# Encoder layer, second FFN matrix: a block that leaves later, a gate inside an operand, and a last row block in two half banks

## The chip, the cores and the metric

The kernel runs on one core of a Trainium2 chip. The metric is the device time of one execution in microseconds (us). Five engines have queues of their own: PE multiplies matrices, ACT and DVE work elementwise and read PE's banks, POOL works elementwise on SBUF, and SP issues all the transfers that matter here. PEld in the rows is PE's loading of weights.

## The reference

One encoder layer: conditioning by six modulation rows, two attention branches, a gated merge, and then the part that the change touches. With `h2` the modulated norm of `x`:

```
a, up = jnp.split(h2 @ w_ffn_in[l], 2, axis=-1)
x = x + gt2 * ((jax.nn.silu(a) * up) @ w_ffn_out[l])
```

`x` is 1024 x 1024, the inner width D_FF is 2816, `gt2` is one row of 1024 gates that multiplies each row. All is float32.

## The kernel before

The products are done in pieces: a float32 operand is split into a rounded part `whi` (copied by ACT, line 107) and the rest `wlo` (subtracted by DVE or POOL, line 108), and three matmuls per pair of operands (hi-hi, hi-lo, lo-hi, `PASS`) make up one product. The function `wsplit` does that for an operand of 128x512; `wload` (line 100) loads one into one of six buffers `raw`. There are ten buffers each for `whi` and `wlo`.

The second FFN matrix, `[silu(a)*up] @ w_ffn_out`, is a 2x2 block product with 7 block products instead of 8. `PRODS` lists them; `prod2(n)` does product n, with n from 0 to 6 here. Each sums over 11 steps k; a step takes an operand a (a combination of the activations, from `ga_d`) and an operand b (a block of the weights or a mix of blocks), and does 4 row blocks m x 3 passes = 12 matmuls of 512 columns, so 132 in a product. The four sums of a product lie in four banks, of the tags `d` and `s` for even products and `v` and `t` for odd ones, two banks to a tag.

Products 0, 1 and 2 use blocks of `w_ffn_out` as they are; DVE subtracts both parts `wlo` for them. During products 1 and 2 `w2_mix(k)` also loads all four blocks of step k again (line 1336) and DVE makes the mixes of them (lines 1338 to 1341), 44 subtractions in all, for products 3 to 6. From product 3 on POOL subtracts most of the `wlo` of operand b. Product 6 uses the fourth mix (`m3` in the program, made in line 1341). Its last three steps (`LASTK`) are done row block by row block, so that the four sums are ready one after the other.

What a product gives is added into four output blocks c11, c12, c21, c22 of four tiles 128x512 each. A block that is ready is finished by `finish`: a load of the residual from `x2_d` (line 1382), a multiplication by the gate on DVE (line 1383), an addition of the residual on POOL (line 1384) and a store (line 1386). c11 is ready after product 1 and is finished there. c21 gets its gate and residual ahead of product 6, which is still missing in it; product 6 is then multiplied by the gate out of its banks and added (lines 1418, 1419), and stored (line 1420).

PE's order is that of the program. The order on ACT, DVE, POOL and SP is made by a scheduler when the program is built: it takes what is ready in its own timeline, by the order of the program as priority. Each engine then runs its queue strictly in order.

Of the kernel before, what the change touches and what calls it, by code (L numbers as in the profile page):

```python
# [10 lines left out]
F32 = mybir.dt.float32  # L11
# [30 lines left out]
def hybrid_layer(ctx: ExitStack, tc: tile.TileContext, x, colp, wada1, wada2, bada2, wqkv, wg, wpa, wpb,  # L42
                 wo, w1, w2, hgain, ropeg, rope, rbias, bmask, g2r, out):
    nc = tc.nc

    def pool(name, side, **kw):
        return tc.alloc_tile_pool(name=name, bufs=1, side=side, reuse_waits="tile", **kw)
# [19 lines left out]
    def bank(tag):  # L67
        return ps.tile([128, 512], F32, tag=tag, name="ps_" + tag)
# [26 lines left out]
    def fview(ap):  # L95
        return ap.bitcast(F32)

    def wload(src, n):
        raw = wp.tile([128, 512], F32, tag="raw", bufs=NRAW, name="raw")
        nc.sync.dma_start(raw[:, :n], src)  # L100
        return raw[:, :n]

    def wsplit(r, eng=None):
        n = r.shape[1]
        hi = wp.tile([128, 512], F32R, tag="hi", bufs=NHL, name="whi")
        lo = wp.tile([128, 512], F32R, tag="lo", bufs=NHL, name="wlo")
        nc.scalar.activation(hi[:, :n], r, AF.Copy)  # L107
        (eng or nc.gpsimd).tensor_sub(lo[:, :n], r, fview(hi[:, :n]))  # L108
        return hi, lo
# [1113 lines left out]
    cs = {}  # L1223
# [100 lines left out]
    fp = pool("f2", "left")  # L1324
    gt2 = fp.tile(wide, F32, name="gt2")
    nc.sync.dma_start(gt2, mod_d[3072:4096].rearrange("(o n) -> o n", o=1).to_broadcast([128, 1024]))
    def w2blk(r, c, k):
        return w2[(k + HT * r) * 128:(k + HT * r + 1) * 128, c * 512:c * 512 + 512]
# [4 lines left out]
    def w2_mix(k):  # L1333
        b = [w2p.tile([128, 512], F32, name=f"m{n}_{k}") for n in range(4)]
        for z, (r, c) in zip(b, ((0, 0), (0, 1), (1, 1), (1, 0))):
            pin(nc.sync.dma_start(z, w2blk(r, c, k)))
        t1, t3, t2, t4 = b
        nc.vector.tensor_sub(t1, t3, t1)  # L1338
        nc.vector.tensor_sub(t3, t2, t3)  # L1339
        nc.vector.tensor_sub(t2, t2, t1)  # L1340
        nc.vector.tensor_sub(t4, t4, t2)  # L1341
        w2m[k] = t1, t2, t3, t4

    PRODS = ((0, (0, 0)), (1, (1, 0)), (6, (1, 1)), (4, 1), (3, 0), (5, 2), (2, 3))
    LASTK = 3

    def operands(n, k):
        g, m = PRODS[n]
        a = wload(ga_d[g, k], 512)
        b = w2m[k][m] if n > 2 else wload(w2blk(*m, k), 512)  # L1350
        return wsplit(a, nc.vector), wsplit(b, nc.vector if n < 3 or k == HT - 1 or (n == 6 and k > 4) else None)

    def blocks(name):
        return [fp.tile([128, 512], F32, name=f"{name}{m}") for m in range(4)]

    def prod2(n):
        pb = [bank(("ds", "vt")[n % 2][m // 2]) for m in range(4)]
        last = LASTK if n == 6 else 0

        def mm(k, m, o):  # L1360
            for i, (a, b) in enumerate(PASS):
                nc.tensor.matmul(pb[m], o[0][a][:, m * 128:(m + 1) * 128], o[1][b],  # L1362
                                 start=(k == 0 and i == 0), stop=(k == HT - 1 and i == 2))

        for k in range(HT - last):
            o = operands(n, k)
            if n in (1, 2) and k % 2 == n - 1:
                w2_mix((k + (n - 1) * HT) // 2)
            for m in range(4):
                mm(k, m, o)  # L1370
        ops = {k: operands(n, k) for k in range(HT - last, HT)}
        for m in range(4):
            for k in ops:
                mm(k, m, ops[k])
        return pb

    def finish(rh, c, z, last=None):
        cs = slice(c * 512, c * 512 + 512)
        for m in range(4):
            t = rh * 4 + m  # L1380
            xt = fp.tile([128, 512], F32, tag="x2", bufs=4, name="x2")
            nc.sync.dma_start(xt, x2_d[t * 128:(t + 1) * 128, cs])
            nc.vector.tensor_mul(z[m], z[m], gt2[:, cs])
            nc.gpsimd.tensor_add(z[m], z[m], xt)
            if last is None:
                nc.sync.dma_start(out[t * 128:(t + 1) * 128, cs], z[m])

    c11, c12, c21, c22 = (blocks(z) for z in ("c11", "c12", "c21", "c22"))
    add = nc.vector.tensor_add
    p1 = prod2(0)  # L1390
    for m in range(4):
        nc.scalar.activation(c21[m], p1[m], AF.Copy)
    p2 = prod2(1)
    for m in range(4):
        add(c11[m], c21[m], p2[m])  # L1395
    finish(0, 0, c11)
    p3 = prod2(2)
    for m in range(4):
        add(c12[m], c21[m], p3[m])
    p6 = prod2(3)  # L1400
    for m in range(4):
        add(c21[m], c21[m], p6[m])
        add(c12[m], c12[m], p6[m])
    p5 = prod2(4)
    for m in range(4):
        add(c22[m], c21[m], p5[m])
# [6 lines left out]
    finish(1, 1, c22)  # L1413
    finish(1, 0, c21, True)
    p4 = prod2(6)
    for m in range(4):
        tm = fp.tile([128, 512], F32, tag="tm", bufs=4, name="tmf")
        nc.vector.tensor_mul(tm, p4[m], gt2[:, :512])
        nc.vector.tensor_add(tm, tm, c21[m])
        nc.sync.dma_start(out[(m + 4) * 128:(m + 5) * 128, :512], tm)  # L1420
    w2p.release()
    fp.release()
    ps.release()
# [102 lines left out]
```

## Time and profile before

| | |
|---|---|
| median of 3 runs | 1542.0 us (1538.08 to 1543.08) |
| the profiled execution's own time | 1540.34 us |
| its span, first to last instruction | 1538.5 us |
| granted TensorE clock, mean | 0.999 of full |
| busy | PE 98%, DVE 72%, ACT 44%, POOL 35% |

The trace has a time for each instruction of one execution. Times are counted from the span's start; a row gives the start, the length, the engine, the line of the program and the tiles it writes and reads. Where an engine stood idle before an instruction, the row ends with how long and with what ended it. PE's matmuls overlap, so their starts tell the pace, not their lengths.

### The profile page before, as it was taken

How to read it: one execution, taken by the hardware profiler on the slowest of the kernel's cores; microseconds unless marked ns; L12 is line 12 of the kernel's file. 1: busy time of each engine (PE TensorE's matmuls, PEld its weight loads, DVE VectorE, ACT ScalarE, POOL GpSimd, SP SyncE). 2: the span in 40 equal slices, each digit the busy share in tenths (PEclk: the TensorE clock that was granted, in tenths of full speed). 3: DMA queues.
4: the chain of work that ended last, by engine and by line, in shares of the span. 5: the costliest groups of instructions: out<-in, count | busy, mean ns of one | idle time of the engine just before them, and what ended most of it. 6: DMA issues, size and time to landing. Idle time of an engine off the chain costs nothing. (4 is left out here: it accounts for less than half of the span.)

```text
span 1538.5 us, 24632 instructions
## 1 busy us (share of the span) xinstructions
PE 1513.6 (98%) x8156; PEld 1268.2 (82%) x8156; DVE 1109.3 (72%) x2428; ACT 671.3 (44%) x1719; POOL 531.8 (35%) x540
## 2 busy tenths in 40 slices
PE   9999999999999999999999999999999999999998
PEld 7988898988888877788888888888888888887886
DVE  6867786776889855466665497788767775599468
ACT  5555654555555453245532344233233333344442
POOL 0422331321000030001361211677777775104464
PEclk9999999999999999999999999999999999999999
DMA  9615355552354354833553235345443334798342
GB/s 366 231 47 177 106 160 163 172 170 83 104 149 131 107 172 138 299 120 117 171 169 139 86 105 179 112 135 178 156 132 103 107 111 131 256 357 284 104 151 103
DMA packets 158016, 241.67 MB, mean 157 GB/s; under 512 B 27312, under 2 KB 77360, under 8 KB 157120
## 3 DMA queue, kind: packets, MB, share of 16 engines
q1 hardware_dynamic: 156736, 235.90, 47.0%
q10 hardware_dynamic: 1152, 4.19, 0.7%
q8 instruction: 65, 1.06, 0.3%
q14 instruction: 63, 0.52, 0.1%
HBM read 179.89 MB, written 60.15 MB: 156 GB/s over the span
## 5 line engine op out<-in xcount | busy, mean ns | idle before, releaser
L107 ACT ACTIVATE whi<-raw 128x512 fp32r<-128x512 f32 (+1 forms) x348 | 205.0, 601 | 300.5 <-PE ps_s L1362 40.6
L108 POOL TENSOR_TENSOR wlo<-raw,whi 128x512 fp32r<-128x512 f32 (+2 forms) x133 | 168.9, 1282 | 473.1 <-ACT whi L107 323.8
L292 PE MATMUL ps_d<-whi,hT 128*128 128x384 f32 x1152 | 317.5, 343 | 1.3 <-ACT v L327 1.3
L108 DVE TENSOR_TENSOR wlo<-raw,whi 128x512 fp32r<-128x512 f32 (+1 forms) x215 | 184.3, 868 | 79.3 <-ACT whi L107 74.6
L292 PEld LDWEIGHTS ps_d<-whi,hT 128*128 128x128 f32 x1152 | 211.0, 188 | 7.0 <-ACT vs L330 2.6
L292 PE MATMUL ps_d<-wlo,hT 128*128 128x384 f32 x576 | 193.9, 337 | 0.4 <-POOL wlo L108 0.4
L292 PEld LDWEIGHTS ps_d<-wlo,hT 128*128 128x128 f32 x576 | 108.8, 189 | 0.7 <-POOL wlo L108 0.7
L107 ACT ACTIVATE whi<-ws 128x512 fp32r<-128x512 f32 x65 | 41.0, 631 | 123.9 <-DVE ws L1209 47.4
L1142 POOL TENSOR_TENSOR e<-e,c 128x512 f32<-128x512 f32 x44 | 68.2, 1549 | 66.3 <-DVE c L1272 40.3
L322 POOL TENSOR_TENSOR ra<-qn,rtab 128x64 f32<-128x64 f32 x48 | 16.8, 349 | 170.8 <-DVE qn L315 144.0
L456 ACT ACTIVATE P<-P,st 128x256 f32<-128x256 f32 (+2 forms) x100 | 46.1, 462 | 58.5 <-DVE st L455 58.5
L108 POOL TENSOR_TENSOR wlo<-m,whi 128x512 fp32r<-128x512 f32 x35 | 51.9, 1493 | 54.6 <-ACT whi L107 54.5
L599 PE MATMUL ps_d<-hT,whi 128*128 128x512 f32 x192 | 60.5, 396 | 0.0
L1192 PE MATMUL ps_v<-h2T,whi 128*128 128x512 f32 x192 | 59.3, 390 | 0.0
L1192 PE MATMUL ps_s<-h2T,whi 128*128 128x512 f32 x192 | 59.2, 390 | 0.0
L456 ACT ACTIVATE P<-P,sx 128x384 f32<-128x384 f32 (+1 forms) x64 | 37.1, 580 | 48.0 <-DVE sx L455 48.0
L441 PE MATMUL ps_s<-qk 64*128 64x256 f32 (+3 forms) x492 | 53.8, 321 | 3.3 <-DVE qk L371 2.0
L1192 PE MATMUL ps_d<-h2T,whi 128*128 128x512 f32 x184 | 56.9, 390 | 0.0
L313 DVE TENSOR_REDUCE ss<-sq 128x4 f32<-128x256 f32 x80 | 33.1, 414 | 32.6 <-ACT sq L310 32.5
L441 PEld LDWEIGHTS ps_s<-qk 64*128 64x128 f32 (+1 forms) x492 | 35.0, 182 | 25.2 <-issue 13.2
L482 PE MATMUL ps_v<-PT,v 128*64 128x128 f32 (+1 forms) x672 | 54.6, 284 | 0.8 <-DVE PT L471 0.8
L108 DVE TENSOR_TENSOR wlo<-ws,whi 128x512 fp32r<-128x512 f32 x45 | 49.4, 1098 | 8.2 <-ACT whi L107 8.2
(436 smaller groups left out, 3989.6 us busy)
## 6 DMA issues: line engine op xcount, KB each, us to landing
raw<-in_w_dram SPq DMA_DIRECT2D x139, 256.0 KB
ga_d<-e SPq DMA_DIRECT2D x77, 256.0 KB
raw<-ga_d SPq DMA_DIRECT2D x77, 256.0 KB
wa<-in_wada_dram SPq DMA_DIRECT2D x32, 512.0 KB
raw<-in_wqkv_dram SPq DMA_DIRECT2D x80, 192.0 KB
m<-in_w_dram SPq DMA_DIRECT2D x44, 256.0 KB
raw<-in_wg_dram SPq DMA_DIRECT2D x42, 256.0 KB
xt<-in_x_dram SPq DMA_DIRECT2D x16, 512.0 KB
```

Of the source, the lines that this page charges most:

```text
L107: nc.scalar.activation(hi[:, :n], r, AF.Copy)
L108: (eng or nc.gpsimd).tensor_sub(lo[:, :n], r, fview(hi[:, :n]))
L292: nc.tensor.matmul(pd[:, :384], tok(a, k, t), U.w[k][b][:, :384], start=(k == 0 and i == 0), stop=(k == KT - 1 and i == 2))
L313: nc.vector.tensor_reduce(ss, sq.rearrange("p (h d) -> p h d", h=4), axis=mybir.AxisListType.X, op=ALU.add)
L322: nc.gpsimd.tensor_tensor(v4(ra), v4(qn[:, :, 0:16]), tv(0, 0, 16), op=ALU.mult)
L441: nc.tensor.matmul(I.pS[h][:nq, :nk], U.qk[a][hs, I.q0:I.q0 + nq], U.qk[2 + b][hs, I.kb0 * 128:I.kb0 * 128 + nk], start=(i == 0), stop=(i ...
L456: nc.scalar.activation(P[:nq, :nk], P[:nq, :nk], AF.Exp, scale=-1.0, bias=nm, accum_out=sm)
L482: nc.tensor.matmul(po[hs, :nq], U.v[:, I.kb0 + i, hs], I.PT[h][:, i, :nq], start=(i == 0), stop=(i == nkb - 1))
L599: nc.tensor.matmul(st["p"], gw[i, br][j][a][:, kk * 128:(kk + 1) * 128], hT[b][:, k, hs], start=(k == 0 and q == 0), stop=(k == 7 and q == 2))
L1142: nc.gpsimd.tensor_mul(sg, sg, up)
L1192: nc.tensor.matmul(pb, w[p][:, k * 128:(k + 1) * 128], b[q][:, k], start=(k == 0 and i == 0), stop=(k == 3 and i == 2))
```

## The change

It makes three edits in the second FFN matrix. `finish(0, 0, c11)` is written after product 3's additions instead of after product 1's. Operand b of product 6 is multiplied by the gate before it is split, 11 multiplications of 128x512 on DVE; the four multiplications of product 6's banks by the gate go, and its banks are added straight into c21. The fourth row block of product 6 is summed as two halves of 256 columns in two banks, the second of the tag `v`, with an addition and a store each. Lines below the edits move by 5 to 7.

```diff
     def operands(n, k):
         g, m = PRODS[n]
         a = wload(ga_d[g, k], 512)
         b = w2m[k][m] if n > 2 else wload(w2blk(*m, k), 512)
+        if n == 6:
+            nc.vector.tensor_mul(b, b, gt2[:, :512])
         return wsplit(a, nc.vector), wsplit(b, nc.vector if n < 3 or k == HT - 1 or (n == 6 and k > 4) else None)
...
         last = LASTK if n == 6 else 0
-
-        def mm(k, m, o):
+        whole = slice(0, 512)
+        cuts = [(m, whole, pb[m]) for m in range(4)]
+        if last:
+            pb.append(bank("v"))
+            cuts[3:] = [(3, HALF[h], pb[3 + h][:, HALF[h]]) for h in range(2)]
+
+        def mm(k, m, o, cs, p):
             for i, (a, b) in enumerate(PASS):
-                nc.tensor.matmul(pb[m], o[0][a][:, m * 128:(m + 1) * 128], o[1][b],
+                nc.tensor.matmul(p, o[0][a][:, m * 128:(m + 1) * 128], o[1][b][:, cs],
                                  start=(k == 0 and i == 0), stop=(k == HT - 1 and i == 2))
...
-            for m in range(4):
-                mm(k, m, o)
+            for m, cs, p in cuts:
+                mm(k, m, o, cs, p)
...
-    finish(0, 0, c11)
     p3 = prod2(2)
...
         add(c21[m], c21[m], p6[m])
         add(c12[m], c12[m], p6[m])
+    finish(0, 0, c11)
     p5 = prod2(4)
...
     p4 = prod2(6)
-    for m in range(4):
-        tm = fp.tile([128, 512], F32, tag="tm", bufs=4, name="tmf")
-        nc.vector.tensor_mul(tm, p4[m], gt2[:, :512])
-        nc.vector.tensor_add(tm, tm, c21[m])
-        nc.sync.dma_start(out[(m + 4) * 128:(m + 5) * 128, :512], tm)
+    for m, hs, p in [(m, slice(0, 512), p4[m]) for m in range(3)] + [(3, HALF[h], p4[3 + h]) for h in range(2)]:
+        add(c21[m][:, hs], c21[m][:, hs], p[:, hs])
+        nc.sync.dma_start(out[(m + 4) * 128:(m + 5) * 128, hs], c21[m][:, hs])
```

How the queues move. First DVE at the start of product 2, before the change. The tiles `c_15030` to `c_15033` are c11, `gt` is the gate, `m_7` and its like are the mixes of step 7:

```order
L1395 TENSOR_TENSOR c_15030<-c_15038,ps_v 128x512
L108 TENSOR_TENSOR wlo<-raw,whi 128x512
L1395 TENSOR_TENSOR c_15031<-c_15039,ps_v 128x512
L108 TENSOR_TENSOR wlo<-raw,whi 128x512
L1383 TENSOR_TENSOR c_15030<-c_15030,gt_15025 128x512
L1395 TENSOR_TENSOR c_15032<-c_15040,ps_t 128x512
L108 TENSOR_TENSOR wlo<-raw,whi 128x512
L1395 TENSOR_TENSOR c_15033<-c_15041,ps_t 128x512
L1383 TENSOR_TENSOR c_15031<-c_15031,gt_15025 128x512
L108 TENSOR_TENSOR wlo<-raw,whi 128x512
L1338 TENSOR_TENSOR m_7_15782<-m_7_15783,m_7_15782 128x512
L1383 TENSOR_TENSOR c_15032<-c_15032,gt_15025 128x512
```

And the same place with the change, where line 1383 has become 1390 and 1395 has become 1402:

```order
L1402 TENSOR_TENSOR c_15031<-c_15039,ps_v 128x512
L108 TENSOR_TENSOR wlo<-raw,whi 128x512
L1390 TENSOR_TENSOR c_15030<-c_15030,gt_15025 128x512
L1402 TENSOR_TENSOR c_15032<-c_15040,ps_t 128x512
L108 TENSOR_TENSOR wlo<-raw,whi 128x512
L1402 TENSOR_TENSOR c_15033<-c_15041,ps_t 128x512
L108 TENSOR_TENSOR wlo<-raw,whi 128x512
L1352 TENSOR_TENSOR m_6_15705<-m_6_15705,gt_15025 128x512
L1390 TENSOR_TENSOR c_15031<-c_15031,gt_15025 128x512
L1338 TENSOR_TENSOR m_7_15762<-m_7_15763,m_7_15762 128x512
L1390 TENSOR_TENSOR c_15032<-c_15032,gt_15025 128x512
L108 TENSOR_TENSOR wlo<-raw,whi 128x512
```

The multiplications of c11 by the gate stand where they stood, and one of the eleven new ones (line 1352) stands among them.

Second, DVE at the end of product 2, where the mixes of the last step are made; before the change:

```order
L1338 TENSOR_TENSOR m_10_15962<-m_10_15963,m_10_15962 128x512
L1339 TENSOR_TENSOR m_10_15963<-m_10_15964,m_10_15963 128x512
L1340 TENSOR_TENSOR m_10_15964<-m_10_15964,m_10_15962 128x512
L1341 TENSOR_TENSOR m_10_15965<-m_10_15965,m_10_15964 128x512
L108 TENSOR_TENSOR wlo<-raw,whi 128x512 x3
L1399 TENSOR_TENSOR c_15034<-c_15038,ps_d 128x512
```

With the change:

```order
L1338 TENSOR_TENSOR m_10_15942<-m_10_15943,m_10_15942 128x512
L1339 TENSOR_TENSOR m_10_15943<-m_10_15944,m_10_15943 128x512
L1340 TENSOR_TENSOR m_10_15944<-m_10_15944,m_10_15942 128x512
L1341 TENSOR_TENSOR m_10_15945<-m_10_15945,m_10_15944 128x512
L108 TENSOR_TENSOR wlo<-raw,whi 128x512
L1352 TENSOR_TENSOR m_10_15945<-m_10_15945,gt_15025 128x512
L108 TENSOR_TENSOR wlo<-raw,whi 128x512 x2
L1405 TENSOR_TENSOR c_15034<-c_15038,ps_d 128x512
```

The first two `wlo` here are the two parts of product 2's step 10, the third is product 3's; the last of the new multiplications stands between the two. The other ten stand ahead of it, one behind each set of mixes.

Third, the end of DVE's queue, before the change and with it:

```order
L1418 TENSOR_TENSOR tmf<-ps_s,gt_15025 128x512
L1419 TENSOR_TENSOR tmf<-tmf,c_15040 128x512
L1418 TENSOR_TENSOR tmf<-ps_s,gt_15025 128x512
L1419 TENSOR_TENSOR tmf<-tmf,c_15041 128x512
L1522 UNCONDITIONAL_BRANCH
```

```order
L1424 TENSOR_TENSOR c_15039<-c_15039,ps_d 128x512
L1424 TENSOR_TENSOR c_15040<-c_15040,ps_s 128x512
L1424 TENSOR_TENSOR c_15041<-c_15041,ps_s 128x256
L1424 TENSOR_TENSOR c_15041<-c_15041,ps_v 128x256
L1527 UNCONDITIONAL_BRANCH
```

Two operations per row block become one, and the last row block's one becomes two of half the width.

## Rows read from the trace of the kernel before

**Rows 1.** The page's second part: DVE's busy tenths in 40 slices.

```profile
DVE  6867786776889855466665497788767775599468
```

**Rows 2.** Timeline of PE, product 2 (start us, length us, what): start, hole, end.

```profile
1378.20 0.39 PE L1362 MATMUL ps_d<-whi 128*128 128x512 f32 x1
1378.43 0.39 PE L1362 MATMUL ps_d<-wlo,whi 128*128 128x512 f32 x1
...
1392.57 0.50 PE L1362 MATMUL ps_d<-wlo,whi 128*128 128x512 f32 x1 [3.09 <-DVE wlo L108]
...
1410.06 0.50 PE L1362 MATMUL ps_d<-wlo,whi 128*128 128x512 f32 x1
...
1412.72 0.39 PE L1362 MATMUL ps_v<-whi 128*128 128x512 f32 x1
```

**Rows 3.** Windows: length, then PE, PEld, DVE, ACT, POOL, clock, DMA share, GB/s.

```profile
1342.00:1378.00 36.00, 36.00 (x161) 29.80 (x160) 32.74 (x51) 15.61 (x26) 0.00 (x0) 1.00 1.01 363
1378.00:1413.00 35.00, 31.56 (x135) 24.63 (x133) 32.98 (x48) 13.55 (x23) 7.21 (x5) 1.00 0.94 331
```

**Rows 4.** Timelines of POOL and DVE in product 2.

```profile
1385.74 1.68 POOL L1384 TENSOR_TENSOR c<-c,x 128x512 f32<-128x512 f32 x1 [1.82 <-DVE c L1383]
...
1386.18 1.78 DVE L1338 TENSOR_TENSOR m<-m,m 128x512 f32<-128x512 f32 x1
...
1394.24 0.68 DVE L1338 TENSOR_TENSOR m<-m,m 128x512 f32<-128x512 f32 x1
1394.84 0.68 DVE L1340 TENSOR_TENSOR m<-m,m 128x512 f32<-128x512 f32 x1
```

**Rows 5.** The same timelines at the seam of products 2 and 3.

```profile
1408.72 1.28 DVE L108 TENSOR_TENSOR wlo<-raw,whi 128x512 fp32r<-128x512 f32 x2
...
1412.71 1.20 DVE L108 TENSOR_TENSOR wlo<-raw,whi 128x512 fp32r<-128x512 f32 x1
...
1412.07 3.00 POOL L108 TENSOR_TENSOR wlo<-m,whi 128x512 fp32r<-128x512 f32 x2 [20.11 <-ACT whi L107]
```

**Rows 6.** Timeline of DVE, products 1 and 2: every idle stretch over 0.2 us.

```profile
1347.82 0.69 DVE L1338 TENSOR_TENSOR m<-m,m 128x512 f32<-128x512 f32 x1 [1.25 <-DMA m<-in_w_dram]
...
1353.13 0.69 DVE L1338 TENSOR_TENSOR m<-m,m 128x512 f32<-128x512 f32 x1 [0.28 <-DMA m<-in_w_dram]
...
1374.67 1.96 DVE L108 TENSOR_TENSOR wlo<-raw,whi 128x512 fp32r<-128x512 f32 x3 [1.17 <-ACT whi L107]
...
1404.57 1.36 DVE L108 TENSOR_TENSOR wlo<-raw,whi 128x512 fp32r<-128x512 f32 x2 [0.25 <-ACT whi L107]
```

**Rows 7.** Waits of SP, 1330 to 1415: total us, times, longest.

```profile
SPq L100 <- DVE wlo L108: 11.3, 17, 1.5
```

**Rows 8.** Timeline at 153 us, scores of one item; then their group (ns of one).

```profile
153.06 0.41 PEld L441 LDWEIGHTS ps_s<-qk 64*128 64x128 f32 x6 [0.25 <-issue]
153.06 0.62 PE L441 MATMUL ps_s<-qk 64*128 64x256 f32 x6
...
L441 PE MATMUL ps_s<-qk 64*128 64x256 f32 x228 | 23.9, 314 | 2.0 <-DVE qk L371 2.0
```

**Rows 9.** Line 1362: weight loads of one kind, ns min/median/max.

```profile
L1362 PEld LDWEIGHTS ps_s<-whi,wlo x88: 187/188/188, 1320.0 to 1533.3; 128*128 128x128 f32 x88
```

**Rows 10.** Timeline of PE and DVE where product 6 begins.

```profile
1503.12 0.39 PE L1362 MATMUL ps_d<-whi 128*128 128x512 f32 x1
...
1503.50 0.68 DVE L1412 TENSOR_TENSOR c<-c,ps_v 128x512 f32<-128x512 f32 x1
```

**Rows 11.** Timeline, the end of the span.

```profile
1533.57 0.39 PE L1362 MATMUL ps_s<-whi,wlo 128*128 128x512 f32 x1
...
1534.00 0.69 DVE L1418 TENSOR_TENSOR tmf<-ps_s,gt 128x512 f32<-128x512 f32 x1 [0.18 <-PE ps_s L1362]
1534.79 0.69 DVE L1419 TENSOR_TENSOR tmf<-tmf,c 128x512 f32<-128x512 f32 x1
```

**Rows 12.** Groups of DVE: 128x256 out of a bank, busy us, mean ns.

```profile
L455 DVE CUSTOM_DVE_ANT_0 P<-ps_s,bmask 128x256 f32<-128x256 f32 x60 | 23.5, 418 | 1.8 <-PE ps_s L441 1.0 <-PE ps_t L467 0.3
```

More of the change, by code (lines that the diff above doesn't have):

```diff
@@ L1344, in hybrid_layer @@
     PRODS = ((0, (0, 0)), (1, (1, 0)), (6, (1, 1)), (4, 1), (3, 0), (5, 2), (2, 3))
-    LASTK = 3
+    LASTK, HALF = 3, (slice(0, 256), slice(256, 512))
     def operands(n, k):
@@ L1368, in prod2 @@
                 w2_mix((k + (n - 1) * HT) // 2)
-            for m in range(4):
-                mm(k, m, o)
+            for m, cs, p in cuts:
+                mm(k, m, o, cs, p)
         ops = {k: operands(n, k) for k in range(HT - last, HT)}
-        for m in range(4):
+        for m, cs, p in cuts:
             for k in ops:
-                mm(k, m, ops[k])
+                mm(k, m, ops[k], cs, p)
         return pb
@@ L1415, in hybrid_layer @@
     p4 = prod2(6)
-    for m in range(4):
-        tm = fp.tile([128, 512], F32, tag="tm", bufs=4, name="tmf")
-        nc.vector.tensor_mul(tm, p4[m], gt2[:, :512])
-        nc.vector.tensor_add(tm, tm, c21[m])
-        nc.sync.dma_start(out[(m + 4) * 128:(m + 5) * 128, :512], tm)
+    for m, hs, p in [(m, slice(0, 512), p4[m]) for m in range(3)] + [(3, HALF[h], p4[3 + h]) for h in range(2)]:
+        add(c21[m][:, hs], c21[m][:, hs], p[:, hs])
+        nc.sync.dma_start(out[(m + 4) * 128:(m + 5) * 128, hs], c21[m][:, hs])
     w2p.release()
```

## Prediction

> **What bounds the kernel now.** The page comes first: DVE, otherwise far from full, reaches nine tenths in two neighbouring slices late in the run [rows 1]; PE is busy throughout. Busy share says little of PE here, because matmuls overlap; the starts do. In the second FFN matrix a 512-column matmul starts about 0.227 us after the one before it (1378.20, 1378.43), so one product of 132 matmuls takes 132 x 0.227 = 29.9 us when nothing is late. Product 2 starts at 1378.20 and product 3 at 1412.72: 34.5 us, so PE lost 4.6 us in it, 3.1 of them in one hole before 1392.57, whose releaser is DVE's `wlo` [rows 2]. Second view, the windows: in the two stretches ahead of product 2 and in it DVE is busy for over 90%, the DMA engines for 94% or more, and PE's clock is granted in full [rows 3]. Product 2 is therefore set by DVE and the loads it shares a loop with, not by PE; products 3 to 5 are PE alone; and behind the last matmul there is a short serial tail. The change touches DVE's stretch and the tail.
>
> **Finishing c11 later: nothing.** In the order of the changed kernel the four multiplications of c11 stand at the same place of DVE's queue, between the parts of product 2, and POOL's four adds are still the first that POOL does in this matrix: the scheduler puts work where its inputs are ready, and the later position in the program moves neither. On SP one store goes behind four loads of mixes and two loads of the residual go a step later; nobody waits for these in product 2, and the number of issues there is the same. I cost it at 0. Its bounds: at the low end, were the block really gone from product 2, DVE would save four multiplications of 0.60 and the slowing by POOL's adds. That slowing shows in the rows: a subtraction that starts at 1386.18 beside the POOL add of 1385.74 takes 1.78 us instead of 0.68 [rows 4], 1.10 more; four such make 4.4, so 6.8 us in all. At the high end nothing is added.
>
> **Eleven multiplications by the gate.** Each is a 128x512 operation from SBUF to SBUF. Independent ones of this form start 0.60 us apart (1394.24, 1394.84) [rows 4], so eleven take 6.6 us. All eleven stand ahead of the last part of product 2 in DVE's queue (the last sits between the two parts of step 10), so all weigh on the matmul that starts at 1410.06, released by the parts that DVE began at 1408.72 [rows 2, 5]. What can hide them is DVE's idle time ahead of that: 1.25 + 0.28 + 1.17 + 0.25 = 2.95 us [rows 6], each ended by a load or by ACT behind a load. If the loads come when they came before, 6.6 - 2.95 = 3.65 us are left, and PE, which at step 10 waits for DVE, loses them in full. That is what I take. The bounds: 0 below, if PE's lead over DVE were larger than the rows say; 6.6 above, if the loads move with DVE. They partly do: SP waited 17 times, 11.3 us in all, for a `wlo` to give a raw buffer back before it could issue a load [rows 7].
>
> **A collision at the seam.** After product 2 the b operands' parts go to POOL, which starts at 1412.07, and the DVE part at 1412.71 beside it takes 1.20 us instead of 0.68 [rows 5]. That was behind step 10. With DVE 3.65 us late, step 10's last operations fall at 1412.4 to 1413.7, into POOL's first subtraction. One more operation is slowed by 1.10 us [rows 4]; I add 1.1. Bounds: 0 if POOL comes equally late, 4.4 if four operations are caught.
>
> **The halves.** Row block 3 of product 6 now takes 33 x 2 matmuls of 256 columns instead of 33 of 512. No row has one of that shape; the nearest is attention's scores, where six 256-column matmuls that alternate between two halves of the array lie in 0.62 us [rows 8]. With the 0.31 us of one taken off, their starts are 0.06 apart, 0.12 for each half of the array, close to half a 512-column start plus 0.01. So a pair costs 0.24 against 0.227: 33 x 0.013 = 0.4 us more, all on PE's path. The upper bound is a weight load that sets the pace: 0.188 us in this matrix [rows 9], so 66 x 0.188 - 33 x 0.227 = 4.9 us. I take 0.4, because the six loads in the scores stand closer than 0.188 apart. The extra bank is free in time: DVE's last read of a `v` bank begins at 1503.50, and product 6, which starts at 1503.12, comes to `v` only after nine whole and three half matmuls, 2.4 us later [rows 10].
>
> The Trainium skill, "TensorE: Matmul & The Clock Gate", section "The mechanism", says that a weight load overlaps matmuls in flight only where its row group differs; here it doesn't differ, and by this each of the 33 loads would add its whole length. The rows disagree: matmuls of 512 columns start 0.227 us apart [rows 2] with a load of 0.188 between each two [rows 9]; were the load not beside a matmul, 512 columns would pass in 0.04 us, while 256 take 0.12 [rows 8].
>
> **The tail.** Before: the last matmul starts at 1533.57, DVE multiplies from 1534.00 and adds until 1534.79 + 0.69 = 1535.48 [rows 11], which is 1.68 us behind the end of that matmul's turn (1533.57 + 0.227). After: one addition of 128x256 out of PSUM. Its start after the turn's end stays at 0.2, its length is that of a 128x256 operation from PSUM, 0.42 us [rows 12]: 0.62, so 1.06 us less. The last store halves to 128 KB; at the 363 GB/s of the windows [rows 3] that is 0.35 us less, the bounds being 0 and 0.7. The other additions of this kind have a whole row block's time to hide in; the first half's add and store lie beside the second half's nine matmuls (1.1 us).
>
> **The sum.** 3.65 + 1.1 + 0.4 - 1.06 - 0.35 = 3.75 us, against the profiled execution's own 1540.34: 1544.1 us. That execution lies 1.7 under the median of the three runs shown, 1542.0, and inside their spread. What a measurement of this kernel can tell from no change is about 0.3%, 4.6 us, so the forecast counts as no change, on its slow side.
>
> **The rivals.**
> - *The lateness feeds itself (slower).* Place: the loop of six raw buffers in products 1 and 2. A late `wlo` frees its buffer late, the load is issued late, ACT's copy comes late, and DVE's idle time stays although it has more work. Then 6.6 stays whole: 6.6 + 1.1 + 0.4 - 1.4 = 6.7, 1547.0; with all four collisions at the seam 1550.3. For it: SP's 17 waits [rows 7], and a DMA share near its limit [rows 3], so that a load can't catch up. Against it: two of the four idle stretches were ended by loads of the mixes, which wait for no raw buffer [rows 6]. It decides when product 3 starts later than about 1419. Chance 0.32.
> - *All hidden.* If the eleven fit beside late loads, only halves and tail are left: 0.4 - 1.4 = -1.0, 1539.3. Against it: step 10 waits for DVE in the rows. Chance 0.14.
> - *The weight load sets the pace of the halves.* 4.9 in place of 0.4: 1548.6. Chance 0.05. The Trainium skill's rule above, at the 0.188 of the rows, would give 33 x 0.188 = 6.2 in place of the 0.4, and 1549.9.
> - *The block does leave product 2*, as the change says: 3.75 - 6.8 gives 1537.3. The order speaks against it. Chance 0.04.
>
> **The numbers.** The forecast has the remaining 0.45. The range takes in the hidden case below and the feeding loop with one collision, and the slow weight load, above: 1538.5 to 1549.0. Left out are the four-collision end and what lies under 1538.5, less than 0.2 together. Slower by over 0.3%: most of the loop rival (0.28), the weight-load rival (0.05) and the upper edge of the forecast (0.09): 0.42. Faster by over 0.3%: the block leaving, with luck: 0.05. Within: 0.53.
>
> **What the changed profile would show.** Right: DVE without idle time over 0.3 us from 1350 to step 10 of product 2; the hole of product 2 longer than 3.1 us or split in two; product 3 starting at 1416 to 1418; matmuls of 256 columns 0.12 apart; one addition of some 0.42 us between the last matmul and the last store. Wrong: product 3 starting at 1413 (hidden), or later than 1419 (the loop); half matmuls 0.19 apart; POOL's first adds in product 3 or later.

## The result and the profile after

| | before | after |
|---|---|---|
| median | 1538.94 us (10 runs, 1536.04 to 1543.08) | 1545.67 us (10 runs, 1541.96 to 1550.53) |
| profiled execution, its span | 1540.34, 1538.5 | 1541.96, 1540.1 |
| product 2, start to start | 34.52 us | 39.60 us |
| product 3 | 30.56 us | 29.92 us |
| product 6's start to the span's end | 35.4 us | 34.4 us |

The ratio is 1.0042, interval 1.0029 to 1.0055: the change makes the kernel slower by 0.4%, 6.7 us between the medians. The forecast was 1544.1 with a range of 1538.5 to 1549.0, which holds the result; of the three outcomes it is the second likeliest (slower by over 0.3%, 0.42) that came.

The profiled execution after is the fastest of its ten, and that of before, a further one, is slower than the median of the ten. The 1.6 us between the two spans therefore says little. Stretches say more: products 2 and 3 together take 4.44 us longer (39.60 + 29.92 against 34.52 + 30.56), and the end is 1.0 shorter.

The page's second part, DVE's tenths in 40 slices (it was [rows 1]): nine tenths are reached in the same two neighbouring slices.

```profile
DVE  6767777776889845466665497788777775599467
```

The windows (length, then PE, PEld, DVE, ACT, POOL, clock, DMA share, GB/s). The first two are the stretches of [rows 3], with product 2 beginning 1.81 us earlier in them; the third is a piece of product 2:

```profile
1342.00:1378.00 36.00, 36.00 (x161) 29.80 (x160) 34.58 (x57) 16.56 (x28) 0.00 (x0) 1.00 1.01 358
1378.00:1413.00 35.00, 28.24 (x115) 22.17 (x113) 34.86 (x48) 14.85 (x25) 9.85 (x7) 0.95 0.90 313
1390.90:1395.00 4.10, 4.03 (x11) 3.18 (x12) 4.10 (x7) 0.63 (x1) 1.14 (x1) 0.58 0.94 331
```

DVE has gone from 32.74 to 34.58 us in the first, and to all but 0.14 us of the second. PE issues 115 matmuls where it issued 135 in the second. In the third PE's granted clock is 0.58; in the windows of [rows 3] it was full.

PE's timeline in product 2 (it was [rows 2]), its start, its holes and product 3's start:

```profile
1376.39 0.39 PE L1369 MATMUL ps_d<-whi 128*128 128x512 f32 x1
...
1390.97 0.51 PE L1369 MATMUL ps_d<-wlo,whi 128*128 128x512 f32 x1 [3.30 <-DVE wlo L108]
...
1392.12 0.63 PE L1369 MATMUL ps_d<-wlo,whi 128*128 128x512 f32 x1
1392.55 0.63 PE L1369 MATMUL ps_d<-whi,wlo 128*128 128x512 f32 x1
...
1413.36 0.50 PE L1369 MATMUL ps_d<-wlo,whi 128*128 128x512 f32 x1 [2.77 <-DVE wlo L108]
...
1415.99 0.39 PE L1369 MATMUL ps_v<-whi 128*128 128x512 f32 x1
```

A third hole, of 1.05 us, lies before 1404.81; all three are released by DVE's `wlo`. Behind the first, matmuls of 512 columns start 0.43 us apart for about 3 us: the lower of the clock's two levels, 1.2 GHz.

DVE's timeline in products 1 and 2: its only idle stretch over 0.2 us (there were four ahead of step 10's parts, [rows 6], and one of 1.50 us behind them that is not listed there), the operations slowed beside c11's additions on POOL, and the seam (it was [rows 5]):

```profile
1351.51 0.69 DVE L1338 TENSOR_TENSOR m<-m,m 128x512 f32<-128x512 f32 x1 [1.05 <-DMA m<-in_w_dram]
...
1381.88 1.46 DVE L108 TENSOR_TENSOR wlo<-raw,whi 128x512 fp32r<-128x512 f32 x1
...
1386.26 1.78 DVE L1390 TENSOR_TENSOR c<-c,gt 128x512 f32<-128x512 f32 x1
1387.96 0.68 DVE L108 TENSOR_TENSOR wlo<-raw,whi 128x512 fp32r<-128x512 f32 x1
1388.56 1.75 DVE L1390 TENSOR_TENSOR c<-c,gt 128x512 f32<-128x512 f32 x1
1390.23 2.96 DVE L108 TENSOR_TENSOR wlo<-raw,whi 128x512 fp32r<-128x512 f32 x3
...
1409.86 1.77 DVE L1352 TENSOR_TENSOR m<-m,gt 128x512 f32<-128x512 f32 x1
1411.56 3.44 DVE L108 TENSOR_TENSOR wlo<-raw,whi 128x512 fp32r<-128x512 f32 x2
```

And POOL's in the same stretch (it was part of [rows 4] and [rows 5]):

```profile
1381.49 1.29 POOL L1391 TENSOR_TENSOR c<-c,x 128x512 f32<-128x512 f32 x1 [50.58 <-issue]
1385.81 1.67 POOL L1391 TENSOR_TENSOR c<-c,x 128x512 f32<-128x512 f32 x1 [3.04 <-DVE c L1390]
...
1409.41 6.75 POOL L108 TENSOR_TENSOR wlo<-m,whi 128x512 fp32r<-128x512 f32 x4 [17.37 <-ACT whi L107]
```

c11's four additions are POOL's first of this matrix, as before: the block did not leave. At the seam three operations of DVE are slowed by about 1.1 us each.

The end of the span (it was [rows 11]):

```profile
1536.31 0.28 PE L1369 MATMUL ps_v<-wlo,whi 128*128 128x256 f32 x1
1536.43 0.28 PE L1369 MATMUL ps_v<-whi,wlo 128*128 128x256 f32 x1
...
1536.75 0.42 DVE L1424 TENSOR_TENSOR c<-c,ps_v 128x256 f32<-128x256 f32 x1 [0.58 <-PE ps_v L1369]
```

Matmuls of 256 columns 0.12 apart, one addition of 0.42, ended at 1537.17, and the span 2.9 behind that (before: 3.0).

### The profile page after: what moved, and what is told of

It reads as the page before. It is cut to its first block, busy times and chain, and to the rows that moved or that the text cites. A ratio compares the mean times of both kernels' runs of the same rounds, so it can differ in the third digit from the quotient of the medians.

```text
span 1540.1 us, 24708 instructions
## 1 busy us (share of the span) xinstructions
PE 1513.5 (98%) x8189; PEld 1270.0 (82%) x8189; DVE 1110.9 (72%) x2436; ACT 670.8 (44%) x1719; POOL 530.5 (34%) x540
## 3 DMA queue, kind: packets, MB, share of 16 engines
q8 instruction: 65, 1.06, 0.3%
## 5 line engine op out<-in xcount | busy, mean ns | idle before, releaser
L107 ACT ACTIVATE whi<-raw 128x512 fp32r<-128x512 f32 (+1 forms) x348 | 205.0, 601 | 303.9 <-PE ps_t L1369 34.4
L467 PE MATMUL ps_t<-ident,P 128*128 128x128 f32 (+1 forms) x336 | 51.6, 274 | 3.6 <-DVE P L459 1.2
```

Source lines behind the costliest of these rows:

```text
L467: nc.tensor.transpose(pt[:, i * 128:i * 128 + nq], P[:nq, i * 128:(i + 1) * 128], ident[:nq, :nq])
```

## Experiments

Theory at the outset: the time goes where the prediction put it, into DVE's queue in product 2, by the eleven multiplications. The rivals: the halves cost it, c11's block costs it, or the transfers that share the loop do. "Loss" below is what products 2, 3 and 4 take beyond 3 x 29.92 us in the profiled execution, by the starts of their first matmuls. "End" is product 6's first matmul to the span's end. The kernels ran in four series, each with runs of before of its own, to which its ratios are taken: the change; the next four rows; the next four, to the change again; the last four. Loss and end of before are from the profile of the first series.

| kernel | median, us | ratio (interval) | loss, us | end, us |
|---|---|---|---|---|
| before | 1538.94 / 1535.61 / 1535.85 / 1536.29 | 1 | 5.24 | 35.4 |
| the change | 1545.67 | 1.0042 (1.0029 to 1.0055) | 9.68 | 34.4 |
| gate alone | 1542.55 | 1.0040 (1.0028 to 1.0052) | 9.03 | 34.6 |
| halves alone | 1536.48 | 1.0002 (0.9988 to 1.0015) | 3.17 | 35.4 |
| c11 held back, alone | 1532.29 | 0.9974 (0.9965 to 0.9984) | 0.00 | 35.5 |
| all held back | 1540.48 | 1.0030 (1.0021 to 1.0040) | 9.50 | 34.4 |
| c11 held, gate spread, halves | 1531.81 | 0.9973 (0.9963 to 0.9983) | 0.00 | 34.4 |
| the same, whole last block | 1531.97 | 0.9974 (0.9966 to 0.9983) | 0.00 | 34.7 |
| c11 held, gate early, halves | 1531.91 | 0.9972 (0.9962 to 0.9981) | 0.89 | 34.4 |
| the change, again | 1541.76 | 1.0041 (1.0029 to 1.0054) | 8.99 | 34.4 |
| c11's multiplications put back | 1535.66 | 0.9985 (0.9970 to 1.0000) | 4.38 | 34.4 |
| POOL's additions put back | 1539.21 | 1.0012 (0.9998 to 1.0027) | 8.24 | 34.4 |
| residual loads put back | 1531.48 | 0.9964 (0.9951 to 0.9976) | 1.73 | 34.4 |
| multiplications and additions put back | 1540.51 | 1.0026 (1.0011 to 1.0040) | 8.25 | 34.4 |

### One part at a time

The gate alone: the multiplications go ahead of the split, and the banks are added straight, each whole.

```diff
+        if n == 6:
+            nc.vector.tensor_mul(b, b, gt2[:, :512])
...
-        nc.vector.tensor_mul(tm, p4[m], gt2[:, :512])
-        nc.vector.tensor_add(tm, tm, c21[m])
+        add(c21[m], c21[m], p4[m])
...
```

> Only the gate goes into operand b of product 6; the block c11 is finished where it was and the last row block stays whole, with one addition of 128x512 behind the last matmul. Theory (DVE's eleven multiplications lengthen product 2, +4 to 5 us, and the tail loses one operation of 0.69 + 0.10): product 2 takes 38.5 to 40 us instead of 34.5, the kernel is 3 to 6 us slower, ratio 1.002 to 1.004. Rival (the halves or the moved block are at fault): product 2 stays at 34.5 us and the kernel is 0.8 us faster.

The ratio is that of the whole change, 1.0040 against 1.0042, and product 2 takes 38.95 us. The call of `finish` stands in its old place here, so the moved call does nothing by itself that can be told.

The halves alone, with the multiplication and addition behind the banks, each on half a row block:

```diff
+            pb.append(bank("v"))
+            cuts[3:] = [(3, HALF[h], pb[3 + h][:, HALF[h]]) for h in range(2)]
...
+        nc.vector.tensor_mul(tm[:, hs], p[:, hs], gt2[:, hs])
+        add(tm[:, hs], tm[:, hs], c21[m][:, hs])
```

> Only the last row block in two halves; the gate is multiplied behind the banks as before, in halves too. Theory (half matmuls start 0.12 us apart and two operations of 0.42 replace two of 0.69): PE +0.4, tail -0.5, store -0.35, so -0.5 us, no measurable change, product 2 at 34.5 us. Rival (the halves cost what the change lost): 3 to 6 us slower, with starts 0.19 apart.

No difference that can be measured. Of the three edits the gate carries the loss.

### Making c11 leave

The order had shown that a later call does not move c11. To hold it back, a dependency is needed: a copy of the gate in a buffer of its own, which one column of c12 marks behind product 3's additions and a load then fills.

```diff
-            nc.vector.tensor_mul(z[m], z[m], gt2[:, cs])
+            nc.vector.tensor_mul(z[m], z[m], gt2[:, cs] if gate is None else gate)
...
-    finish(0, 0, c11)
...
+    mark = fp.tile([128, 512], F32, tag="g2b", bufs=1, name="mark")
+    nc.vector.tensor_copy(mark[:, :1], c12[3][:, :1])
+    g2b = fp.tile([128, 512], F32, tag="g2b", bufs=1, name="g2b")
+    nc.sync.dma_start(g2b, mod_d[3072:3584].rearrange("(o n) -> o n", o=1).to_broadcast([128, 512]))
+    finish(0, 0, c11, gate=g2b)
```

> The kernel before, but c11 does leave two products later: its multiplications take the gate from a second copy that is loaded only after product 3's additions, so the scheduler can't put them earlier. Theory (product 2 is set by DVE, and the block costs it 2.4 us of its own and 4.4 us by POOL's additions beside it): product 2 falls from 34.5 to 30 or 31 us and the kernel is 3 to 4.5 us faster, ratio 0.997 to 0.998. Rival (product 2 is set by the loads, or the collisions with POOL only move): product 2 at 33 to 35 us, no change, or product 4 longer by what product 2 gains.

Products 0 to 5 all take 29.92 us, and the ratio is 0.9974. The same windows as above:

```profile
1342.00:1378.00 36.00, 36.00 (x161) 29.80 (x160) 33.91 (x54) 17.50 (x29) 0.00 (x0) 1.00 1.03 373
1378.00:1413.00 35.00, 35.00 (x156) 29.00 (x155) 31.42 (x47) 16.75 (x29) 9.21 (x6) 1.00 0.84 295
```

PE is busy for all 35.00 us, and the DMA engines, which had seemed as near their limit as DVE, fell to 0.84: product 2 is through at 1407.20, inside the window. The whole stall of product 2 was c11's finish. This also tells what before usually loses there: the two kernels differ in little else, so 1535.61 - 1532.29 = 3.3 us is about the loss of the median execution. The profiled one lost 5.24.

Then all three edits with the late copy as the gate, for c11 and for product 6's operand (`tensor_mul(b, b, g2b)`):

> The change, with the gate of the eleven multiplications and of c11 taken from the copy that comes after product 3. Theory: products 1 and 2 lose all of this work, product 2 takes 30 to 31 us, tail 1.0 us less: 4 to 5.5 us faster than before, ratio 0.9965 to 0.9975. Rival (fifteen multiplications in a row on DVE, slowed by POOL's subtractions beside them, make product 4's operands late): product 4 takes over 31 us and the gain is half or nothing.

Product 2 is whole, and the loss has gone to product 4, which takes 39.42 us, as the rival had it. DVE's and PE's timelines there, and a window on the matmuls behind the hole:

```profile
1444.76 4.70 DVE L1390 TENSOR_TENSOR c<-c,g2b 128x512 f32<-128x512 f32 x4 [2.80 <-DMA g2b<-mod_d]
1449.38 12.01 DVE L1352 TENSOR_TENSOR m<-m,g2b 128x512 f32<-128x512 f32 x9
1461.31 0.68 DVE L108 TENSOR_TENSOR wlo<-raw,whi 128x512 fp32r<-128x512 f32 x1
```

```profile
1462.04 0.80 PE L1369 MATMUL ps_d<-whi,wlo 128*128 128x512 f32 x1 [7.26 <-DVE wlo L108]
```

```profile
1462.00:1466.20 4.20, 4.16 (x10) 3.33 (x11) 4.20 (x7) 0.00 (x0) 0.00 (x0) 0.50 0.43 127
```

Everything that waited for one copy became ready at once, and thirteen multiplications stand in a block, 1.33 us each on average for the nine in the second row, of which six meet a POOL operation, instead of 0.60. PE waits 7.26 us for the `wlo` behind them, and then runs at the lower clock. Held back is not enough; it matters what it is held back to.

### Where the gate may stand

The gate's multiplications one per step of product 3, each tied to that step's operand, with c11 held back as above:

```diff
+        if n == 3:
+            g = fp.tile([128, 512], F32, tag="gk", bufs=2, name="gk")
+            nc.vector.tensor_copy(g[:, :1], a[:, :1])
+            nc.scalar.activation(g, gt2[:, :512], AF.Copy)
+            nc.vector.tensor_mul(w2m[k][3], w2m[k][3], g)
```

> Finishing c11 behind product 3 on a late copy of the gate, halves, additions straight out of the banks, and the eleven gate multiplications one per step of product 3, each held back until that step's operand has landed. Theory (the multiplications cost only where DVE sets the pace, in product 2): products 0 to 5 all take 29.92 us, and against the run with c11 late alone (0.9974) the tail gives 1.06 + 0.1 back and the halves take 0.4, so 0.8 us less: ratio 0.997. Rival (eleven more DVE operations, slowed beside POOL's, cost wherever they stand): product 3 or 4 has a hole of 3 us or more, as product 4 had 9.4 us when fifteen stood in one block, and the ratio is 0.999 or above.

As the theory has it: none of products 0 to 5 loses anything, ratio 0.9973. Beside it the same with the last row block whole:

```diff
-        if last:
-            pb.append(bank("v"))
-            cuts[3:] = [(3, HALF[h], pb[3 + h][:, HALF[h]]) for h in range(2)]
...
+    for m, hs, p in [(m, slice(0, 512), p4[m]) for m in range(4)]:
```

> The run with the spread multiplications, but the last row block whole in one bank, with one addition and one store. Theory: the halves pay 0.4 us in matmuls and give back 0.27 us of the last addition and about 0.1 us of the store, so this is level with the halved one, 0.3 us either way, and the matmuls of row block 3 lie 0.227 apart. Rival (the halves are what makes the tail short): 0.6 us or more slower than with halves.

0.9974: level, as expected in the median. In the profiles the end is 34.7 without halves and 34.4 with them, so they give 0.3 to 0.4 us, too little for the runs to tell; the rival's 0.6 is not reached.

Next the gate as the change has it, in products 1 and 2, and only c11 held back:

> c11 finished late as before, but the eleven gate multiplications where the change has them, in products 1 and 2, with halves. Theory (DVE's time sets product 2): the gate alone made it 38.95 us; the block that leaves takes four multiplications of 0.60 and four slowings of 1.10 with it, 6.8 us, so product 2 takes about 32 us (31 to 34), with holes released by DVE's parts. Rival (what c11's leaving freed was the loads and stores of the finish, not DVE): product 2 takes 29.92 us all the same, and the ratio is that of c11 late alone, 0.997.

0.9972, product 2 takes 29.93 us, product 3 30.80. The theory's 32 us fell, and the rival's number came. So the eleven multiplications alone cost next to nothing, 0.89 us in the profile and nothing that the medians tell; beside c11's finish the loss is 9 us with them and 3.2 to 5.2 without. What is left is released by POOL, in its and PE's timelines:

```profile
1400.56 14.34 POOL L108 TENSOR_TENSOR wlo<-m,whi 128x512 fp32r<-128x512 f32 x7 [70.89 <-ACT whi L107]
```

```profile
1406.02 0.50 PE L1369 MATMUL ps_v<-wlo,whi 128*128 128x512 f32 x1 [0.57 <-POOL wlo L108]
```

And the change itself once more:

> The change as it is, once more beside these. Theory (the 3 us that the median lies above what the profiled execution explains are stretches at a lower granted clock behind the holes, more of them in other executions): the mean clock is lower in the slower executions, 0.001 of it for about 1.5 us, and the profile shows the clock fall behind a hole of about 3 us; ratio 1.004. Rival: the clock stays full in the profile though the time is again 5 us above, and the time lies in longer holes.

1.0041, and the same picture: holes of 3.37, 1.10 and 1.75 us, the lower clock behind the first. The theory of the clock fell: mean clock and time don't go together (1540.96 us at 0.996, 1545.01 at 0.998). In product 2 slow matmuls are free as long as PE comes to wait for DVE again behind them, and it does, twice. The rival fell too, since the clock was not full in the profile. Here the profiled execution, 1541.13, lies near the median, 1541.76; what made the first series' median 3.7 us longer than its profiled execution stays open.

### What of c11's finish it is

Base for all four is the kernel with c11 held, gate early and halves, whose products 2 to 4 lose 0.89 (the expectations have 0.84, read off its holes). First its four multiplications back behind product 1; loads, additions and stores stay late.

```diff
+    for m in range(4):
+        nc.vector.tensor_mul(c11[m], c11[m], gt2[:, :512])
...
+        xt = fp.tile([128, 512], F32, tag="x2", bufs=4, name="x2")
+        nc.vector.tensor_copy(xt[:, :1], c12[m][:, :1])
+        nc.sync.dma_start(xt, x2_d[m * 128:(m + 1) * 128, :512])
+        nc.gpsimd.tensor_add(c11[m], c11[m], xt)
+        nc.sync.dma_start(out[m * 128:(m + 1) * 128, :512], c11[m])
```

> The run with the late c11 and the early gate, and of c11's finish the four multiplications back behind product 1; the residual loads, POOL's additions and the stores stay behind product 3. Products 2 and 3 lost 0.84 us in that run over 2 x 29.92. Theory (DVE's time): four more operations of 0.60 make the loss 0.84 + 2.4 = 3.2 us. Rival (loads and stores of the finish are what filled product 2): the loss stays under 1.2.

The loss is 4.38, more than the theory's 3.2, and not where it said: product 2 takes 29.92, the hole is at product 3's start, and POOL is named. POOL's and PE's timelines, and a window behind the hole:

```profile
1402.18 14.56 POOL L108 TENSOR_TENSOR wlo<-m,whi 128x512 fp32r<-128x512 f32 x6 [74.48 <-ACT whi L107]
```

```profile
1408.94 0.50 PE L1369 MATMUL ps_v<-wlo,whi 128*128 128x512 f32 x1 [2.47 <-POOL wlo L108]
```

```profile
1408.90:1413.00 4.10, 4.06 (x11) 3.28 (x12) 2.46 (x5) 0.08 (x1) 4.10 (x3) 0.61 0.32 106
```

Of the 4.38, 2.62 are the hole and most of the rest is the clock, which costs here because nothing behind it makes PE wait. The ten executions go from 1530.96 to 1537.76 us, three of them below 1532 like the base, so this hole seems not to come each time.

Then only POOL's part: four additions on scratch tiles, c11 added to itself, behind product 1.

```diff
+    for m in range(4):
+        sc = fp.tile([128, 512], F32, tag="x2", bufs=4, name="sc")
+        nc.gpsimd.tensor_add(sc, c11[m], c11[m])
```

> The same base, and instead of the multiplications four additions of POOL behind product 1, on scratch tiles that nobody reads (c11 added to itself), so that only the slowing of DVE's neighbours is added. Theory: four operations of DVE grow by 1.10 each, the loss is 0.84 + 4.4 = 5.2 us. Rival (the slowing falls on operations out of the banks or into idle time, or it is the transfers): under 2 us.

The loss is 8.24 us, more than the theory's 5.2 and nearly that of the change, from four additions of 1.0 to 1.5 us on an idle engine. By the medians it is less: 2.9 us above its before, where the base lies 3.9 below, makes 6.9 us, against 9.9 for the change. DVE's timeline shows how, near the additions and at the seam, and PE's what came of it:

```profile
1384.10 1.15 DVE L1338 TENSOR_TENSOR m<-m,m 128x512 f32<-128x512 f32 x1
1385.17 2.12 DVE L108 TENSOR_TENSOR wlo<-raw,whi 128x512 fp32r<-128x512 f32 x2
...
1404.81 1.79 DVE L108 TENSOR_TENSOR wlo<-raw,whi 128x512 fp32r<-128x512 f32 x1
1406.53 1.75 DVE L1352 TENSOR_TENSOR m<-m,gt 128x512 f32<-128x512 f32 x1
1408.20 4.03 DVE L108 TENSOR_TENSOR wlo<-raw,whi 128x512 fp32r<-128x512 f32 x3
```

```profile
1400.97 0.50 PE L1369 MATMUL ps_d<-wlo,whi 128*128 128x512 f32 x1 [1.53 <-DVE wlo L108]
...
1410.00 0.68 PE L1369 MATMUL ps_d<-wlo,whi 128*128 128x512 f32 x1 [3.30 <-DVE wlo L108]
```

Beside the additions DVE loses 2.4 us (1.3 of it in the first two rows); being late, its last operations of product 2 fall into POOL's `wlo` for product 3 and lose 1.1 + 1.1 + 2.2 = 4.4 more. The seam is the larger part.

The loads of the residual alone, behind product 1:

```diff
+    xe = [fp.tile([128, 512], F32, tag="x2", bufs=4, name="xe") for m in range(4)]
+    for m in range(4):
+        nc.sync.dma_start(xe[m], x2_d[m * 128:(m + 1) * 128, :512])
```

> The same base, and only the four loads of the residual (256 KB each) put behind product 1; multiplications, additions and stores stay behind product 3. Theory (DVE's time): the loss stays at 0.84, 0 to 1.5. Rival (the DMA engines, near 100% busy there, set the pace): 1 MB at 363 GB/s is 2.9 us, a loss of 3.7.

The loss is 1.73, between the two theories and nearer to DVE's; the median, 0.9964, is no worse than without. The hole is again at product 3's start and POOL's, as its and PE's timelines show:

```profile
1400.78 14.49 POOL L108 TENSOR_TENSOR wlo<-m,whi 128x512 fp32r<-128x512 f32 x7 [71.56 <-ACT whi L107]
```

```profile
1406.39 0.50 PE L1369 MATMUL ps_v<-wlo,whi 128*128 128x512 f32 x1 [1.39 <-POOL wlo L108]
```

The loads are not what filled product 2. The stores were not put back by themselves.

Last, multiplications and scratch additions together, without any transfer:

> The four multiplications and the four scratch additions on POOL together, without any transfer of the finish. Theory (DVE's time alone, with the clock behind a hole): 0.84 + 2.4 + 4.4 = 7.6 us, 9.3 if the clock falls behind the first hole as in the change, where the loss was 8.99 to 9.68; ratio 1.002 to 1.003. Rival (the two overlap, or the transfers carry a good part): 5 us or less, ratio below 1.001.

8.25 us and 1.0026, in size what the theory says, by a mechanism that it does not contain. Product 2 takes 29.92 us, and none of DVE's operations in it is slowed. POOL is. Its timeline, DVE's beside it, and PE's:

```profile
1386.57 27.68 POOL L1406 TENSOR_TENSOR sc<-c 128x512 f32<-128x512 f32 x4 [56.02 <-DVE c L1404]
1414.21 6.69 POOL L108 TENSOR_TENSOR wlo<-m,whi 128x512 fp32r<-128x512 f32 x5
```

```profile
1386.95 0.68 DVE L108 TENSOR_TENSOR wlo<-raw,whi 128x512 fp32r<-128x512 f32 x1
1387.55 0.68 DVE L1404 TENSOR_TENSOR c<-c,gt 128x512 f32<-128x512 f32 x1
1388.16 0.68 DVE L108 TENSOR_TENSOR wlo<-raw,whi 128x512 fp32r<-128x512 f32 x1
...
1409.23 0.68 DVE L108 TENSOR_TENSOR wlo<-raw,whi 128x512 fp32r<-128x512 f32 x1
1409.84 1.27 DVE L1409 TENSOR_TENSOR c<-c,ps_d 128x512 f32<-128x512 f32 x2
```

```profile
1415.97 0.80 PE L1369 MATMUL ps_v<-wlo,whi 128*128 128x512 f32 x1 [6.64 <-POOL wlo L108]
```

Four additions that took 1.0 to 1.5 us each with POOL's additions alone take 27.68 us, 24.24 of them the first. From 1386.95 to 1409.23 DVE's operations between SBUF tiles start 0.60 us apart without a break, 38 of them, and POOL's first addition ends only when DVE turns to a bank at 1409.84. Its `wlo` for product 3 comes behind and is late by 6.64 us, and the clock falls again. So this run does not repeat what happens in the change, where POOL's additions went through; that they suffice for most of the loss is shown by the run with them alone.

## Why the prediction was right in sign and short in size

- **What bounds product 2.** Right that it is DVE's stretch and that PE is not the bound, shown by c11 held back. Missed: DVE bounds it there only through its meetings with POOL. Without these even the eleven multiplications fit (loss 0.89), and POOL's additions alone bring most of the loss back.
- **Finishing c11 later: nothing.** Right. Its multiplications and POOL's additions stayed where they were, and the run with the gate alone, where the call is not moved, has the same ratio. The rival in which the block does leave was given 1537.3 against 1540.34, a gain of 3.0; with the block made to leave, the same three parts gave 0.9972, 4 us.
- **Eleven multiplications.** Right in mechanism. DVE's idle time ahead of step 10 went from 2.95 to 1.05 us (the prediction's sign of no stretch over 0.3 us from 1350 on was missed by that one), six of the eleven lay ahead of product 2, and c11's first addition still came 1.28 us behind product 2's start (1.21 before), so these six were absorbed. The other five are 5 x 0.60 = 3.0, where the step had 3.65.
- **A collision at the seam.** Right in place, too small: three operations are caught, (1.77 - 0.68) + (3.44 - 1.28) = 3.25 us, of which two, 2.2 us, lie ahead of what step 10 waits for. The term had 1.1. Together 3.0 + 2.2 = 5.2; step 10's matmul comes 36.97 us behind product 2's start, where it came 31.86: 5.11 later. Product 3 lost 0.64 us before and nothing now, which leaves the 4.44.
- **The halves and the tail.** 0.4 - 1.06 - 0.35 was -1.01; the end is 1.0 shorter. Within it the tail gave its 1.06 (from 1536.43 + 0.12 to 1537.17 are 0.62 us), but the store only about 0.1 (2.9 against 3.0 from the last addition to the end). What made up for that was not foreseen: product 6's own small holes came to 0.24 us instead of 0.71, as also where the halves were made alone (0.26). The half row block then cost -1.0 + 1.06 + 0.1 + 0.47 = 0.6 where 0.4 was put. The matmuls came 0.12 apart; the pace of the weight load, 0.188, did not come.
- **The sum and its base.** By stretches the profiles differ by 4.44 - 1.0 = 3.4, where the sum said 3.75: the seam's 1.1 too little, the multiplications' 0.65 too much and the 0.64 that product 3 gave back nearly cancel, which is luck. The medians differ by 6.7. The step that failed is the one ahead of the sum: it was set upon a profiled execution that lost 5.24 us in products 2 and 3, as if that were the usual loss, and its difference to the median of three was passed over as lying in their spread. The median loss of before is about 3.3, from the run with c11 held back. That of the change is about 1541.76 - 1531.81 = 9.95, against the run with the spread gate and the same end, which loses nothing; the forecast had 5.24 + 3.65 + 1.1 = 9.99. So the median moves by 9.95 - 3.3 - 1.0 = 5.7; measured were 5.9 in that series and 6.7 in the first. Of the 3 us that the forecast is short of the 6.7, 1.9 are thus the base; the rest, most of it the 0.8 between the two series, stays open. That 1544.1 came within 1.6 of the measured 1545.67 is luck in part: 1540.34 lay 1.4 above the median of the ten runs of before.
- **The rival of the feeding loop** had priced 6.7, but it is not what happened: its mark was that DVE's idle time stays, and it went; product 3 was to start later than 1419 and started at 1415.99, or 1417.80 with the 1.81 us by which product 2 began earlier in this profile. And the loads by themselves cost little.

## What to carry to other kernels

A later line of the program moved nothing here, where a scheduler takes what is ready; a dependency did, and it should spread what it releases over the steps rather than release it at once. Where DVE and POOL both work on SBUF tiles, four short additions on an otherwise idle POOL can cost more than their own time (5.4 us of additions; 7.4 of loss here in the profiles, 6.9 by the medians), so look first at what POOL could do elsewhere, and at the seam where POOL's next share begins. Here c11 held back gives 0.26% alone; gate and halves on top of it add nothing that these runs can tell.

## What the runs showed that was not expected

**POOL can be shut out for long.** When a POOL operation and DVE operations between SBUF tiles met, one of two things happened: POOL's went on and one DVE operation took up to 1.78 us instead of 0.68 (before, the change, POOL's additions alone), or DVE went on at 0.60 and POOL stood: its first operation then took 24.24 us with multiplications and additions put back, and 5.41, 6.71 and 5.56 us in the three runs where six or seven `wlo` took over 14 us. The Trainium skill, "SBUF — State Buffer", section "SBUF: two separate sides", says that a DVE operation with two inputs in SBUF and a POOL operation that reads SBUF share a pair of ports, that whichever starts first has it for its whole instruction and that the other is blocked meanwhile. The rows agree that one of them stands; but POOL stood through 38 DVE operations and not one. The traces show one difference: in these four cases the operation was POOL's first after 56 to 74 us of idle time and met DVE operations that followed each other without a break, while every other POOL operation of this matrix, in all fourteen traces, took at most 1.86 us. Among these are some that met such a row after 0.6 to 18.5 us of idle time, as at the seam of the change (17.37). Whether the idle time decides it is open: no run varied it by itself.

**A hole can cost more than its length.** In the profiles PE's granted clock fell to the lower level behind holes of 3.30 (the first of the change), 2.47 and 7.26 us, and matmuls started 0.43 apart for about 3 to 4 us; behind the hole of 3.09 in before [rows 2] and that of 2.77 in the change it did not, and with c11 held back, without holes, it stayed at 1.00. With c11's multiplications put back, where nothing later makes PE wait, that is most of 4.38 - 2.62 = 1.8 us; in the change, where PE comes to wait for DVE again, it is nothing as far as the rows tell.

**A profiled execution can be off in just the stretch that is argued on.** Before lost 5.24 us in products 2 and 3 in its profiled execution, 3.3 in the median; the kernel with halves alone, the same in that stretch, lost 3.17.
